# Reloaded products placed earlier, early operands split together, loads of phase two reordered, last norms a stretch later, in a one-layer hybrid trunk

## The chip, the cores and the metric

The kernel runs on one core of a Trainium2 chip. The metric is device time in microseconds (us) of one execution, taken as the median of several. The engines are TensorE (PE; its weight loads are listed apart as PEld), VectorE (DVE), ScalarE (ACT), GpSimd (POOL) and SyncE (SP, which issues most of the DMAs). Each engine works through its own instructions in the order in which they were written; engines wait for each other by semaphores.

## What is computed

The reference is one decoder layer on 1024 tokens of width 1024. Four mixer groups (convolution, latent attention, pooling, spatial gating) make up the first third of the time and are not touched. What matters here is the end:

```python
h = h + mixed @ w_out[l]
f = jnp.square(jax.nn.relu(rms_norm(h, ffn_norm_g[l]) @ w_ff1[l]))   # 1024 x 4096
h = h + f @ w_ff2[l]                                                # 1024 x 1024
return rms_norm(h, final_norm_g)
```

## The kernel before

**Precision.** Every float32 operand is split into a high part (ACT copies it to the format that TensorE reads) and a low part (DVE subtracts the high part from the value). A product takes three passes: high x high, high x low, low x high (`mm3`).

**Seven products instead of eight.** Both matrix products of the MLP are done in 2x2 blocks with seven block products (Strassen's scheme in Winograd's form). The tokens fall into a first and a second half, the 1024 features into two halves, and the 32 tiles of the hidden layer into 16 *pairs* (`Pair`, weights `a11`, `a12` from the first tile of a pair, `a21`, `a22` from the second). The seven products of a pair are P1 to P7. One product is four blocks of features by three passes, 12 matmuls of 128x512; I call these 12 matmuls a **stretch**.

**The order by hand.** All of the MLP is a list `steps` of `Step` objects, one stretch each, put out by `run` (L887 on) in a fixed order, the queue order of every engine. In turn `k` of its loop come, in this order: the loads of step `k+8`; the `post` of step `k-1` (what is done with its result); `prep(k+4)`, that is the high halves on ACT, then the low halves on DVE, then the operand sums of step `k+4`; the functions in the list `now` of step `k`; the `split` of step `k-1` (a result split into halves and stored); the `pre` of step `k`; and the matmuls of step `k`. So operands are made four stretches ahead, and ACT or DVE standing still in a turn hold up all that they have to do in later turns.

**Early pairs.** While the last attention blocks run, only the first half of the tokens is ready. So for the first 12 pairs (`NEARLY`) P1 and P2 are done first (`Pair.early`, L980 on): `one` computes P1 with `a11` into a PSUM bank `ffe`; its `post` copies it to the tile `m` (two buffers, tag `M`) and stores it to DRAM (`m1[p]`); `two` adds P2 with `a12` into the same bank; its `post` makes the square of the ReLU (`fe`), which is stored whole and, split into halves (`fst`), a second time. The order is one(0), one(1), two(0), one(2), two(1), and so on, so that two(p) follows one(p) three steps later. `a11` and `a12` lie in one raw tile `w_raw` of 512 KB (tag `raw`, two buffers). The split operands `wop` and the stored halves `fst` share ten slots (tag `w`). In the same turns the sums and differences of the second half of the tokens are made, in `now` of the steps 7 to 22 (`hn_T1`, `hn_T1_split`, `combine`, `combine_split`, four of each; `hn_T1` also puts eight transposes on PE, tile `htb`).

**Pairs.** Then come the other five products of pairs 0 to 11, in the order P6(p), P3(p), P7(p), P5(p+1), P4(p). P6, P7 and P4 add up in a PSUM bank `ffx` (tag `W`, two banks), which begins with the stored P1: `load_m1` brings it back to the tile `s1` (tag `e`, one buffer) and `seed` (L1009) copies it into the bank on ACT. P5 and P3 add up in a bank `ffy`. The `post` of P5 keeps it as `s5` (tag `N`, one buffer), that of P6 keeps its bank as `s2` before P7 adds to it, that of P7 adds `s5` and stores, that of P4 takes ReLU and square. Pairs 12 to 15 have all seven products in a row and need no stored P1.

**Phase two.** The second matrix product (`Chunk`, L1086 on) has four chunks of four pairs, each with M1, M2, M4, M6, M5, M7, M3 in this order, and each of these with four token tiles in the order `JS` = 0, 2, 1, 3: 28 stretches a chunk. M1, M6 and M7 use banks `ffa`, the others `ffb`. After each stretch DVE adds the bank to a tile of `h` (`add_h`, L1080). M1, M2 and M4 take stored halves (loads 0, 1, 3 into `fop`), the others sums of the whole values (`f1`, `f2` into `raw_f`); `w1`, `w2` are the weights (`raw_b`). All of these loads are issued by SP, in `now` of some step. The second half of `h` waits in DRAM meanwhile (`h_away`, `h_back`).

**Last norms.** `final(t)` (L1234 on) makes the last norm of a token tile: square and sum on ACT, mean and power -0.5 on POOL, product with factor and gain on DVE, store. In the last chunk M7 finishes tiles 4 to 7, M3 tiles 0 to 3; `final` stands in the `post` of those steps. The very last stretch (`final_tile`) is cut into two quarters of 256 columns, the second of which writes the same bank as the first and so waits for DVE's sum of the first.

The lines of the profile that come up: L160 all matmuls of `mm3`; L878 and L881 high and low half of an operand; L130 and L131 those of a stored result; L977 the copies `m`, `s2`, `s5`; L1011 the seed; L946 ReLU; L948 its square on DVE; L967, L1015, L1102, L1108 the loads of `w_raw`, `s1`, `fop`, `raw_b` and `raw_f`; L1018 to L1027 the sums of a pair's weights; L1237 to L1241 the last norm.

Of the kernel before, what the change touches and what calls it, by code (L numbers as in the profile page):

```python
# [7 lines left out]
F32 = mybir.dt.float32  # L8
# [7 lines left out]
P = 128  # L16
# [61 lines left out]
def _trunk(tc, nc, act, dve, pool, pe, sb, ps, hbm, a):  # L78
# [768 lines left out]
    def slot(name):  # L847
        return wslot(name).rearrange("p (x c) -> p x c", x=2)

    def E(name):  # L850
        return sb.tile([P, 512], F32, tag="e", name=name, bufs=1)

# [75 lines left out]
            nc.sync.dma_start(hs[t], h[4 + t])  # L928

    def h_back():  # L930
        for t in range(4):
            h[4 + t] = U("P", "h_back", [D])
            nc.sync.dma_start(h[4 + t], hs[t])

# [26 lines left out]
    class Pair:  # L961
# [18 lines left out]
        def early(self):  # L980
            p = self.p
            o1, o2 = self.op("a11"), self.op("a12")

            def one():
                self.bx = (W, K, W, O)[p % 4]("ffe")
                mm_half(self.bx, o1.t, "B11", True)

            def one_post():
                self.keep("m1", lambda n: M(n, [512]), self.bx)
                pool.dma_start(m1[p], self.m1)  # L990

            def two():
                mm_half(self.bx, o2.t, "B21", False)

            def two_post():
                self.f = (E if p % 2 == 0 and p < NEARLY - 4 else N)("fe")
                f_relu(p, 0, self.bx, self.f, True)

            def two_split():
                f_parts(p, 0, self.f, slot("fst") if p > 2 else  # L1000
                        sb.tile([P, 2, 512], F32R, tag="CS", name="fst", bufs=1))

            return (Step(one, [o1], loads=[lambda: self.load(0)], post=one_post),
                    Step(two, [o2], post=two_post, split=two_split))

        def banks(self):
            self.bx = W("ffx")
# [21 lines left out]
        def steps(self):  # L1029
            p, whole = self.p, self.p >= NEARLY  # L1030
            S = {}

            def product(name, wop, bank, tok, start, **kw):
                o = self.op(wop)
                S[name] = Step(lambda: mm_half(bank(), o.t, tok, start), [o], **kw)

            def y0():
                self.by = (K, O)[p % 2]("ffy")
                return self.by

            def x():
                return self.bx

            def z_seed():
                self.bz = X("ffz")[:, 0:512]
                if p < NEARLY + 2:
                    set_bank(self.bz)
                act.activation(self.bz, self.bx, AF.Copy)

            def two_post():  # L1050
                self.f11 = E("f11")
                f_relu(p, 0, self.bz, self.f11, False)

            def four_post():
                self.f21 = M("f21", [512])
                f_relu(p, 1, self.bx, self.f21, False)

            load = [lambda: self.load(0, "H"), lambda: self.load(1)]
            if whole:
                product("P1", "a11", x, "B11", True, loads=load, pre=self.banks, post=z_seed, sums=[self.sum1])  # L1060
                load = []
                product("P2", "a12", lambda: self.bz, "B21", False, sums=[self.sum4], post=two_post,
                        split=lambda: f_parts(p, 0, self.f11, slot("fst")))
            product("P5", "a21", y0, "T1", True, loads=load, sums=[self.sum2],
                    post=lambda: self.keep("s5", N, self.by))
            product("P6", "a11", x, "T2", False, pre=None if whole else self.seed, sums=[] if whole else [self.sum4],
                    post=lambda: self.keep("s2", lambda n: M(n, [512]), self.bx))
            product("P3", "a12", lambda: self.by, "B22", False, sums=[] if whole else [self.sum3],
                    post=lambda: f_sum(p, 2, self.by, self.s2))
            product("P7", "a21", x, "T3", False, post=lambda: f_sum(p, 3, self.bx, self.s5),  # L1070
                    split=lambda: f_parts(p, 3, self.s5, slot("fst")))
            product("P4", "a22", x, "T4", False, post=four_post, split=lambda: f_parts(p, 1, self.f21, slot("fst")))
            if whole:
                S["P2"].sums.append(self.sum3)
            self.S = S
# [8 lines left out]
    class Chunk:  # L1084
# [65 lines left out]
        def steps(self, nxt, first):  # L1150
            S = {}
            for m, (bank, start, f, w, to) in self.SPEC.items():
                wops = [Op(w_slot, lambda w=w, i=i: self.r[w, i]) for i in range(NCH)]
                fops = [Op(lambda: unit("B", "fop"), lambda f=f, i=i: self.r[f, i]) for i in range(NCH)]

                def fop(i, f=f, fops=fops):
                    return self.r[f, i] if isinstance(f, int) else fops[i].t

                for n, j in enumerate(JS):
                    def pre(m=m, bank=bank, n=n):  # L1160
                        if n == 0 and m in ("M1", "M2", "M4", "M5"):
                            self.banks(bank)

                    def mm(bank=bank, start=start, j=j, fop=fop, wops=wops):
                        for i in range(NCH):
                            mm3(getattr(self, bank)[j], lambda x: fop(i)[:, x, j * P:(j + 1) * P],
                                lambda y: wops[i].t[:, y, :], start and i == 0, i == NCH - 1, not start)

                    def post(m=m, bank=bank, j=j, n=n, to=to):
                        for t, half in to:  # L1170
                            add_h(t + j, half, getattr(self, bank)[j])
                        if self.last and m == "M7" and n < 2:
                            final(4 + j)
                        if self.last and m == "M3":
                            final(j)
                            if n < 2:
                                final(4 + JS[n + 2])

                    if self.last and m == "M3" and n == 3:
                        mm = lambda fop=fop, wops=wops: final_tile(fop, wops, self.B[3])  # L1180
                        post = None
                    S[m, n] = Step(mm, [wops[n]] + ([] if isinstance(f, int) else [fops[n]]), pre=pre, post=post)
# [6 lines left out]
            for n in range(4):  # L1189
# [7 lines left out]
                now(*ahead_4[n], self.sum("S2", n))  # L1197
                now("M6", n, self.sum("T3", n))
                now("M5", n, self.sum("S4", n))
                now("M1", n, self.ld(1, n))  # L1200
                now("M2", n, self.ld(3, n))
                if nxt:
                    now("M4", n, nxt.ld(0, n))
# [4 lines left out]
    def final_tile(fop, wops, b):  # L1208
# [3 lines left out]
        for n, (lo, hi) in enumerate(pieces):  # L1212
            if n:
                sl = slice(lo - 512, hi - 512)
                for i in range(NCH):
                    mm3(b[:, sl], lambda x: fop(i)[:, x, t * P:(t + 1) * P], lambda y: wops[i].t[:, y, sl],
                        False, i == NCH - 1, True)
                add_h(t, 1, b[:, sl], lo - 512, hi - 512)
            act.activation(jk[:, lo:hi], h[t][:, lo:hi], AF.Square, accum_out=ssq[:, n:n + 1])  # L1219
            pool.tensor_scalar(ms[:, n:n + 1], ssq[:, n:n + 1], 1.0 / D, epsr[:, t:t + 1] if n == 0 else ms[:, n - 1:n],  # L1220
                               ALU.mult, ALU.add)
# [9 lines left out]
        fin["g"] = sb.tile([P, D], F32, tag="CS", name="gain_fin", bufs=1)  # L1231
        nc.sync.dma_start(fin["g"], a["fin_g"].partition_broadcast(P))

    def final(t):  # L1234
        jk = M("fjunk", [512]).bitcast(BF16)
        ssq = small(1, "mssq")
        act.activation(jk, h[t], AF.Square, accum_out=ssq)  # L1237
        ms, rs = small(1, "mr_ms"), small(1, "mr_rs")
        pool.tensor_scalar(ms, ssq, 1.0 / D, epsr[:, t:t + 1], ALU.mult, ALU.add)  # L1239
        pool.tensor_tensor(rs, ms, nhalf[:, 0:1], ALU.pow)  # L1240
        dve.scalar_tensor_tensor(h[t], h[t], rs, fin["g"], ALU.mult, ALU.mult)  # L1241
        nc.sync.dma_start(a["out"][t], h[t])


# [231 lines left out]
    for p in range(NPAIR):  # L1476
# [6 lines left out]
            steps.append(s["P4"])  # L1483
        else:
            steps += [s[n] for n in ("P1", "P5", "P6", "P2", "P7", "P3", "P4")]
        if p + 1 < NEARLY:
            steps[-3 if p + 2 < NEARLY else -2].now.append(pairs[p + 1].load_m1)
    steps[2 * NEARLY - 6].now.append(pairs[0].load_m1)
    tail, tail2 = steps[-7:], steps[-14:-7]
    c0 = chunks[0]  # L1490
    for t, n, name, ii in ((tail2, 1, "w1", (0, 1)), (tail2, 5, "w1", (2,)), (tail, 2, "w1", (3,)),
                           (tail, 2, 0, range(4)), (tail, 3, "w2", range(4)), (tail, 5, "f1", range(4)), (tail, 6, "f2", range(4))):
        t[n].now += [c0.ld(name, i) for i in ii]
    for n in range(4):
        tail[3 + n].now.append(c0.sum("T1", n))
    for c, ch in enumerate(chunks):
        steps += ch.steps(chunks[c + 1] if c + 1 < len(chunks) else None, c == 0)
    steps[-28 * len(chunks) + 3].now.append(h_back)
    steps[-20].now.append(load_gain)
    run(steps)  # L1500


# [105 lines left out]
```

## Time and profile before

| what | us |
|---|---|
| median of 3 runs (lowest, highest) | 1131.64 (1131.16, 1134.97) |
| the profiled execution, its own time | 1135.26 |
| its span, first to last instruction | 1133.5 |
| mean granted TensorE clock | 0.957 of full speed |
| early pairs, from the second `m` copy to the first seeded product | 395.8 to 500.1 |
| pairs 0 to 11, from P6(0) to P6(11) | 500.1 to 696.2 |
| phase two | 786.0 to 1133.5 |

A row of a timeline gives start, duration, engine, line of the kernel, operation, output <- inputs, shapes and number, and in brackets how long the engine had stood idle before it and what ended that wait. A row of a wait list gives the total, the number of times and the longest. PE's durations overlap, since a matmul begins before the one ahead of it has ended: the start of the next row tells the pace.

### The profile page before, as it was taken

Reading aid. Unit: us, or ns where it says so; the run is one execution under the profiler, and the core shown is the slowest. Engines: PE = TensorE matmul, PEld = TensorE weight load, DVE = VectorE, ACT = ScalarE, POOL = GpSimd, SP = SyncE. Lnnn points to the kernel's source line nnn. Section 1 sums busy time; section 2 is a strip of 40 time slices with the busy share of each in tenths; the row PEclk is TensorE's granted clock in tenths of the full one; section 3 lists DMA queues with packets and bytes.
Section 4 is the critical chain, followed back from the end, with each engine's and each line's share of the span. In section 5 each row is a group of like instructions: output and inputs, shape, how many; then the busy total and the mean of one; then the engine's idle time right before and its main releaser. Section 6 shows DMA issues by size and latency. Waiting matters only on the chain. (4 is left out here: it accounts for less than half of the span.)

```text
span 1133.5 us, 13377 instructions
## 1 busy us (share of the span) xinstructions
PE 1016.8 (90%) x4674; PEld 830.9 (73%) x4674; DVE 848.0 (75%) x1276; ACT 499.9 (44%) x936; POOL 245.0 (22%) x333
## 2 busy tenths in 40 slices
PE   9977799999999996667878878999799999999993
PEld 7866688878888885546766666888588888888872
DVE  5999999988887546655546555567698988988874
ACT  7552266566577644444344343554143241431422
POOL 0478666213323221111111111112000000000002
PEclk9998899999999998879899899999899999999996
DMA  9311034101010054845454545458929248166002
GB/s 343 116 48 45 19 105 169 39 19 38 1 57 1 1 184 148 319 165 178 169 179 180 186 159 184 177 194 336 413 81 356 105 152 298 71 236 228 1 37 112
DMA packets 49492, 165.71 MB, mean 146 GB/s; under 512 B 6032, under 2 KB 7952, under 8 KB 49424
## 3 DMA queue, kind: packets, MB, share of 16 engines
q1 hardware_dynamic: 36288, 119.68, 30.0%
q0 software_dynamic: 12992, 45.10, 10.4%
q8 instruction: 37, 0.61, 0.2%
q14 instruction: 31, 0.25, 0.1%
q10 hardware_dynamic: 144, 0.07, 0.0%
HBM read 113.45 MB, written 51.38 MB: 145 GB/s over the span
## 5 line engine op out<-in xcount | busy, mean ns | idle before, releaser
L160 PE MATMUL ffb<-wop,fop 128*128 128x512 f32 (+1 forms) x780 | 185.7, 399 | 19.1 <-DVE h L1080 11.1
L160 PE MATMUL ffx<-hnT,wop 128*128 128x512 f32 x624 | 162.1, 412 | 41.4 <-ACT ffx L1011 40.6
L160 PEld LDWEIGHTS ffb<-wop,fop 128*128 128x128 f32 x780 | 147.7, 193 | 55.5 <-DVE h L1080 11.3
L881 DVE TENSOR_TENSOR wop<-w_raw,wop 128x512 fp32r<-128x512 f32 x112 | 77.0, 689 | 144.8 <-ACT wop L878 144.7
L160 PEld LDWEIGHTS ffx<-hnT,wop 128*128 128x128 f32 x624 | 123.0, 199 | 74.1 <-ACT ffx L1011 45.7
L160 PE MATMUL ffa<-wop,fop 128*128 128x512 f32 x576 | 136.9, 397 | 2.0 <-DVE h_back L1080 2.0
L160 PEld LDWEIGHTS ffa<-wop,fop 128*128 128x128 f32 x576 | 109.3, 190 | 27.7 <-DVE h_back L1080 2.4
L878 ACT ACTIVATE wop<-raw_b 128x512 fp32r<-128x512 f32 x96 | 59.4, 623 | 127.8 <-PE ffa L160 40.0
L878 ACT ACTIVATE wop<-w_raw 128x512 fp32r<-128x512 f32 x112 | 69.7, 625 | 80.9 <-DMA w_raw<-in_w_ff 34.2
L337 DVE SCALAR_TENSOR_TENSOR acc<-ycv,cols,acc 128x512 f32<-128x512 f32 (+22 forms) x100 | 97.0, 1012 | 0.7 <-ACT acc L317 0.4
L160 PE MATMUL ffe<-hnT,wop 128*128 128x512 f32 x288 | 77.2, 425 | 20.3 <-ACT m L977 20.3
L160 PEld LDWEIGHTS ffe<-hnT,wop 128*128 128x128 f32 x288 | 57.8, 205 | 36.4 <-ACT m L977 23.7
L1239 POOL TENSOR_SCALAR mr_ms<-mssq,epsr 128x1 f32<-128x1 f32 x7 | 3.9, 564 | 322.3 <-ACT fjunk L1237 322.1
L878 ACT ACTIVATE fop<-raw_f 128x512 fp32r<-128x512 f32 x64 | 39.8, 623 | 76.4 <-DVE h_back L1080 27.6
L881 DVE TENSOR_TENSOR wop<-raw_b,wop 128x512 fp32r<-128x512 f32 x96 | 65.5, 683 | 5.5 <-ACT wop L878 5.0
L955 POOL DMA_DIRECT2D fs<-fst x48 | 25.9, 539 | 103.6 <-DVE fst L131 100.1
L160 PE MATMUL ffy<-hnB,wop 128*128 128x512 f32 x192 | 47.2, 395 | 0.0
L160 PE MATMUL ffy<-hnT,wop 128*128 128x512 f32 x192 | 46.5, 391 | 0.0
L881 DVE TENSOR_TENSOR fop<-raw_f,fop 128x512 fp32r<-128x512 f32 x64 | 43.8, 685 | 0.0
L937 POOL DMA_DIRECT2D fr<-s x32 | 17.3, 542 | 121.1 <-DVE s L942 121.1
L160 PEld LDWEIGHTS ffy<-hnB,wop 128*128 128x128 f32 x192 | 36.8, 192 | 8.4
L160 PEld LDWEIGHTS ffy<-hnT,wop 128*128 128x128 f32 x192 | 36.0, 188 | 7.9
(448 smaller groups left out, 2167.7 us busy)
## 6 DMA issues: line engine op xcount, KB each, us to landing
fs<-fst POOLq DMA_DIRECT2D x48, 512.0 KB, 3.6
fop<-fs SPq DMA_DIRECT2D x48, 512.0 KB, 7.1
w_raw<-in_w_ff SPq DMA_DIRECT2D x44, 512.0 KB, 4.7
raw_b<-in_w_ff SPq DMA_DIRECT2D x32, 512.0 KB, 5.4
raw_f<-fr SPq DMA_DIRECT2D x32, 512.0 KB, 5.6
fr<-s POOLq DMA_DIRECT2D x32, 256.0 KB, 2.3
fr<-f POOLq DMA_DIRECT2D x20, 256.0 KB, 2.4
xin<-in_x SPq DMA_DIRECT2D x8, 512.0 KB, 8.8
```

Of the source, the lines that this page charges most:

```text
L160: pe.matmul(out, lhs(x), rhs(y), start=start and i == 0, stop=stop and i == 2, skip_group_check=more)
L337: dve.scalar_tensor_tensor(aa, ya, c, aa, ALU.mult, ALU.add)
L878: act.activation(self.t[:, 0], self.src(), AF.Copy)
L881: dve.tensor_sub(self.t[:, 1], self.src(), high(self.t))
L937: pool.dma_start(fr[p][q // 2][:, (q % 2) * 512:(q % 2 + 1) * 512], f)
L955: pool.dma_start(fs[p][q], t.rearrange("p x c -> p (x c)").bitcast(F32))
L1239: pool.tensor_scalar(ms, ssq, 1.0 / D, epsr[:, t:t + 1], ALU.mult, ALU.add)
```

## The change

Six things change:

- An early pair's two operands, `a11` and `a12`, are both operands of `one`; `two` has none. So both are split in the same turn, four stretches ahead of `one`.
- `seed` of pair p moves from the `pre` of its own P6 to `now` of P7 of pair p-1 (pair 0: to `now` of its P5). `load_m1` of pair p moves from `now` of P7(p-1) to `now` of P4(p-2) (pair 1: to P6(0)).
- `s5` of odd pairs goes to a second buffer (tag `CS`) by a new function `spare`.
- The four loads of kind 1 of the first chunk are issued in `tail[3]` (P2 of the last pair), ahead of the four of `w2`, instead of one in each step of M1. `h_back` goes from M1's last step to M2's last, that is behind the loads of kind 3, and in the order `JS`.
- `final` is cut in two: `final_sum` (ACT and POOL) in the turn in which the tile is finished, after that turn's operands, and `final_out` (the product and the store), one turn or more later.
- Tile 4's product goes to ACT and POOL instead of DVE; those of tiles 2 and 1 stand inside `final_tile`, each behind the sum of a quarter.

```diff
+    def spare(name):
+        return sb.tile([P, 2, 512], F32, tag="CS", name=name, bufs=1)[:, 0]
...
     def h_back():
-        for t in range(4):
+        for t in JS:
...
-            return (Step(one, [o1], loads=[lambda: self.load(0)], post=one_post),
-                    Step(two, [o2], post=two_post, split=two_split))
+            return (Step(one, [o1, o2], loads=[lambda: self.load(0)], post=one_post),
+                    Step(two, post=two_post, split=two_split))
...
-                    post=lambda: self.keep("s5", N, self.by))
-            product("P6", "a11", x, "T2", False, pre=None if whole else self.seed, sums=[] if whole else [self.sum4],
+                    post=lambda: self.keep("s5", (N, spare)[p % 2], self.by))
+            product("P6", "a11", x, "T2", False, sums=[] if whole else [self.sum4],
...
-                        if self.last and m == "M7" and n < 2:
-                            final(4 + j)
-                        if self.last and m == "M3":
-                            final(j)
-                            if n < 2:
-                                final(4 + JS[n + 2])
...
-                now("M1", n, self.ld(1, n))
+                if not first:
+                    now("M1", n, self.ld(1, n))
                 now("M2", n, self.ld(3, n))
...
                 add_h(t, 1, b[:, sl], lo - 512, hi - 512)
+                final_out((2, 1)[n - 1])
...
-    def final(t):
+    def final_sum(t):
         jk = M("fjunk", [512]).bitcast(BF16)
         ssq = small(1, "mssq")
         act.activation(jk, h[t], AF.Square, accum_out=ssq)
-        ms, rs = small(1, "mr_ms"), small(1, "mr_rs")
+        ms, fin[t] = small(1, "mr_ms"), small(1, "fin_rs", 4)
         pool.tensor_scalar(ms, ssq, 1.0 / D, epsr[:, t:t + 1], ALU.mult, ALU.add)
-        pool.tensor_tensor(rs, ms, nhalf[:, 0:1], ALU.pow)
-        dve.scalar_tensor_tensor(h[t], h[t], rs, fin["g"], ALU.mult, ALU.mult)
+        pool.tensor_tensor(fin[t], ms, nhalf[:, 0:1], ALU.pow)
+
+    def final_out(t, shared=False):
+        if shared:
+            act.activation(h[t], h[t], AF.Copy, scale=fin[t])
+            pool.tensor_tensor(h[t], h[t], fin["g"], ALU.mult)
+        else:
+            dve.scalar_tensor_tensor(h[t], h[t], fin[t], fin["g"], ALU.mult, ALU.mult)
         nc.sync.dma_start(a["out"][t], h[t])
...
-        if p + 1 < NEARLY:
-            steps[-3 if p + 2 < NEARLY else -2].now.append(pairs[p + 1].load_m1)
     steps[2 * NEARLY - 6].now.append(pairs[0].load_m1)
+    pairs[0].S["P5"].now.append(pairs[0].seed)
+    for p in range(1, NEARLY):
+        (pairs[0].S["P6"] if p == 1 else pairs[p - 2].S["P4"]).now.append(pairs[p].load_m1)
+        pairs[p - 1].S["P7"].now.append(pairs[p].seed)
...
-                           (tail, 2, 0, range(4)), (tail, 3, "w2", range(4)), (tail, 5, "f1", range(4)), (tail, 6, "f2", range(4))):
+                           (tail, 2, 0, range(4)), (tail, 3, 1, range(4)), (tail, 3, "w2", range(4)),
+                           (tail, 5, "f1", range(4)), (tail, 6, "f2", range(4))):
...
-    steps[-28 * len(chunks) + 3].now.append(h_back)
+    steps[-28 * len(chunks) + 7].now.append(h_back)
     steps[-20].now.append(load_gain)
+
+    for k, t in ((-7, 4), (-6, 6), (-5, 5), (-4, 7), (-3, 0), (-2, 2)):
+        steps[k - 1].split = lambda t=t: final_sum(t)
+    for k, t in ((-5, 4), (-4, 6), (-3, 5), (-2, 7), (-1, 0)):
+        steps[k].now.append(lambda t=t: final_out(t, t == 4))
+    steps[-2].split = lambda: final_sum(1)
```

## The prediction

> **What bounds the kernel now.** I read the page's first two parts, then what TensorE waited for, then a table by stage.
>
> ```profile
> span 1133.5 us, 13377 instructions
> ## 1 busy us (share of the span) xinstructions
> PE 1016.8 (90%) x4674; PEld 830.9 (73%) x4674; DVE 848.0 (75%) x1276; ACT 499.9 (44%) x936; POOL 245.0 (22%) x333
> ```
>
> TensorE (PE) is the bound on average, so only its waits are worth anything. The list of waits, from the last mixer products on (total, times, longest):
>
> ```profile
> PE ffx L160 <- ACT ffx L1011: 40.6, 12, 9.0
> PE ffe L160 <- ACT m L977: 20.3, 8, 5.4
> PE ffb L160 <- DVE h L1080: 11.1, 1, 11.1
> PE ffb L160 <- DMA fop<-fs: 8.0, 1, 8.0
> PE ffa L160 <- DVE h_back L1080: 2.0, 1, 2.0
> ```
>
> These five are 82.0 us, and each is touched by one part of the change. The windows by stage (length, then busy us of PE, PEld, DVE, ACT, POOL, then granted clock, DMA share, GB/s):
>
> ```profile
> 395.80:500.10 104.30, 75.79 (x308) 59.39 (x308) 63.10 (x101) 48.17 (x87) 19.98 (x37) 0.89 0.57 206
> 500.10:696.20 196.10, 164.46 (x661) 130.65 (x661) 105.94 (x164) 75.66 (x132) 29.21 (x54) 0.94 0.51 177
> ...
> 786.00:830.20 44.20, 36.18 (x145) 28.53 (x144) 32.22 (x51) 12.63 (x23) 1.62 (x3) 0.88 0.86 347
> 830.20:1086.90 256.70, 256.70 (x1105) 207.52 (x1104) 229.44 (x356) 82.66 (x148) 0.00 (x0) 1.00 0.47 166
> 1086.90:1133.50 46.60, 26.15 (x109) 20.73 (x107) 24.34 (x32) 12.59 (x26) 9.10 (x18) 0.76 0.23 91
> ```
>
> The fourth row is what is possible: 92 stretches in 256.7 us, 2.79 each, at clock 1.00. In the other four TensorE waits and its clock is lower; a wait costs itself and some slow matmuls behind it.
>
> **Part 1, early pairs: both operands split together.**
>
> ```profile
> 395.81 14.10 PE L160 MATMUL ffe<-hnT,wop 128*128 128x512 f32 x60 [0.75 <-ACT m L977]
> 409.75 1.03 PE L793 MATMUL htb<-ident,h 128*128 128x128 f32 x8
> ...
> 446.82 0.63 ACT L878 ACTIVATE wop<-w_raw 128x512 fp32r<-128x512 f32 x1 [4.94 <-DMA w_raw<-in_w_ff]
> ...
> 447.49 0.69 DVE L881 TENSOR_TENSOR wop<-w_raw,wop 128x512 fp32r<-128x512 f32 x1 [3.54 <-ACT wop L878]
> ...
> 453.15 0.69 DVE L948 TENSOR_TENSOR fe<-fe 128x512 f32<-128x512 f32 x1
> ...
> 477.98 0.60 ACT L977 ACTIVATE m<-ffe 128x512 f32<-128x512 f32 x1 [4.17 <-DMA m<-m]
> ...
> 484.72 0.60 ACT L977 ACTIVATE m<-ffe 128x512 f32<-128x512 f32 x1 [0.44 <-DMA m<-m]
> ...
> 495.81 0.63 ACT L878 ACTIVATE wop<-w_raw 128x512 fp32r<-128x512 f32 x1 [1.36 <-DVE w_raw L1018]
> ...
> 500.11 4.73 PE L160 MATMUL ffx<-hnT,wop 128*128 128x512 f32 x12 [8.98 <-ACT ffx L1011]
> ```
>
> ACT stands 4.94 us on a weight load, and behind it, in order, is the copy `m` for which TensorE waits. The load is late because the two raw buffers are freed only when the second operand is split, in the loop turn before the one that needs the next load. Split together, the buffer is free three turns earlier and the load has four turns, some 11 us: this wait goes. No instruction is added; ten operand slots are enough by count (seven held, one or two for the stored products).
>
> What is late next is DVE: 447.49 to 453.84 is ten operations without a gap, 6.3 us for two stretches, against 2 x 2.76 plus 0.8 of transposes, 6.3, on TensorE (five stretches from 395.81 to 409.75 give 2.79). So in the turns with the first hidden-half sums they are even; in the last four pairs of turns DVE has nine to eleven operations, 6.4 to 7.6 us against 5.5, and the copy `m` can meet its buffer still being stored (the 4.17). I put the lag by the last `m` at 8 us (estimate: 4 x about 1.2, and one or two waits of half of 4.17). Dense, TensorE would reach that point at 395.81 + 20 x 2.757 + 4 x 0.8 = 454.1, so the last `m` comes at about 462.5 and not 484.72. Bounds: 454.1, and 484.7 with no gain.
>
> From there to the first `ffx` product it was 15.4 us (500.11 - 484.72). The seed now follows the operand at 495.81 at once: 495.81 + 0.53 + 0.59 gives 497.0 in that frame, 12.3 after `m`. So that product starts at 474.8 and not 500.1: **25 us** gained, bounds 33 and 3.
>
> **Part 2, the seeds, the second s5 buffer.**
>
> ```profile
> 521.56 2.91 PE L160 MATMUL ffy<-hnB,wop 128*128 128x512 f32 x12
> ...
> 529.83 2.88 PE L160 MATMUL ffx<-hnT,wop 128*128 128x512 f32 x12
> 535.58 3.03 PE L160 MATMUL ffx<-hnT,wop 128*128 128x512 f32 x12 [2.87 <-ACT ffx L1011]
> ...
> 552.49 5.49 PE L160 MATMUL ffx<-hnT,wop 128*128 128x512 f32 x12 [2.87 <-ACT ffx L1011]
> ```
>
> ```profile
> 531.40 0.60 ACT L977 ACTIVATE s<-ffy 128x512 f32<-128x512 f32 x1 [2.04 <-DMA fr<-s]
> ...
> 532.74 0.60 ACT L946 ACTIVATE f<-ffx 128x512 f32<-128x512 f32 x1 [0.22 <-PE ffx L160]
> ...
> 534.95 0.58 ACT L1011 ACTIVATE ffx<-s 128x512 f32<-128x512 f32 x1
> ```
>
> Three stretches from 521.56 to 529.83 are 2.757 each. P4 ends near 532.6; ACT then does ReLU, square, an operand and the store's high half, and only then the seed at 534.95, for which P6 waits: 2.87 us in every pair, now and then with a slow stretch behind (5.49). The seed moves to the turn of P7 of the pair before, three turns ahead of its P6. It needs the other of two W banks, read last by ReLU one period back, and `s1` loaded:
>
> ```profile
> s<-m SPq DMA_DIRECT2D x12, 256.0 KB, 4.5
> ```
>
> The one `s1` buffer is free when the previous seed is done, and the load stands in SP's queue behind no load that waits longer; it has almost a period, 13.8 us, for 4.5. So P6 starts at once. Next late would be the copy `s2` between P6 and P7: ACT's four operations after P4 ended by 534.95 without the seed, 2.3 us into a stretch of 2.76, so it is in time. Behind the waiting seed on ACT would be operands four turns ahead, so its own 0.58 is hidden. The second `s5` buffer takes away the 2.04, but ReLU then began 0.22 after TensorE anyway: 0 as long as ACT has this 0.2 us, and at most 2 a pair if not.
>
> Eleven periods of five stretches are 151.6 us and were 196.1: 44.5, of which I keep **44** (bounds 44.5, and 33 if 1 us a pair comes back).
>
> **Part 3, first loads of phase two.**
>
> ```profile
> 771.54 0.33 SPq L1108 DMA_DIRECT2D raw_b<-in_w_ff  x1
> ...
> 805.06 25.33 PE L160 MATMUL ffb<-wop,fop 128*128 128x512 f32 x96 [8.02 <-DMA fop<-fs]
> ```
>
> ```profile
> 800.00:804.00 4.00, 0.00 (x0) 0.00 (x0) 1.90 (x3) 0.63 (x1) 0.00 (x0) 0.59 1.03 420
> ```
>
> M2 waits 8.02 us for four loads at the end of the queue, and runs slow behind it. Dense, M1, M2 and M4 would take 12 x 2.79 = 33.5 of the 44.2: 10.7 to gain. But the DMA engines are full (share 1.03, 420 GB/s): reordering moves the lateness. Before M2 now stand 13 loads of 0.52 MB and about 3 MB of stores, 9.8 MB from 771.5 on: at 420 GB/s, 23.4, and a little slower at first, 797; the last operand behind it 798.5, so M2 waits 1 to 2 us. Eight loads for the sums (4.2 MB, 10 us) and four for M4 (2.1 MB, 5 us) end at 812, when M2 would be done at 810. So some 2.5 us come back there: M6 at 824 and not 830.2, **6 us** (bounds 10.7 and 0). `h_back` moves behind these four loads and lands by 818, its first tile (JS order) by 813.5; M4's first sum needs it at 815.
>
> **Part 4, last norms.**
>
> ```profile
> 1101.90 10.26 PE L160 MATMUL ffb<-wop,fop 128*128 128x512 f32 x48
> 1123.22 2.93 PE L160 MATMUL ffb<-wop,fop 128*128 128x256 f32 x12 [11.07 <-DVE h L1080]
> ```
>
> ```profile
> 1115.18 1.28 DVE L1241 SCALAR_TENSOR_TENSOR h<-h,mr_rs,gain_fin 128x1024 f32<-128x1024 f32 x1 [2.27 <-POOL mr_rs L1240]
> ...
> 1126.19 0.48 DVE L1080 SCALAR_TENSOR_TENSOR h<-ffb,rs,h 128x256 f32<-128x256 f32 x1 [3.02 <-PE ffb L160]
> ```
>
> DVE stands 2.27 us in each norm for the chain square, mean, power, so the sum that the last 256-column product waits for comes 11.07 us late; the 2.0 before the last M7 tile (list of waits) is the same queue. A turn later the factor is there: DVE has one or two sums of a half tile, some 0.75 each (below twice the 0.48 of a quarter), and 1.28 of a norm in a stretch of 2.79. From 1086.93: seven stretches to 1106.5, 1.4 for the first quarter, DVE free at 1108.7 (a sum and a norm from 1106.5), its sum 0.5, the last product 1.4 and 0.2, so its sum begins at 1110.9 and not 1126.19. Behind it the same 7.3 us to the end, plus 0.6 where a norm on DVE holds the last mean on POOL, as here:
>
> ```profile
> 1109.00 1.30 POOL L1239 TENSOR_SCALAR mr_ms<-mssq,epsr 128x1 f32<-128x1 f32 x1
> ...
> 1120.55 0.27 POOL L1239 TENSOR_SCALAR mr_ms<-mssq,epsr 128x1 f32<-128x1 f32 x1 [3.33 <-ACT fjunk L1237]
> ```
>
> (1.30 beside a norm on DVE, 0.27 without.) So 1118.8: **14.5 us** (bounds 16 and 10). Tile 4's norm goes to ACT and POOL; nearest is POOL's 128x1024 subtraction, 3.00 us, off the path if DVE is free of it.
>
> ```profile
> L148 POOL TENSOR_TENSOR wo_1l<-wo_raw,wo_1h 128x1024 fp32r<-128x1024 f32 x2 | 6.0, 2998 | 2.7 <-ACT wo_1h L147 2.7
> ```
>
> [...]
>
> **Sum.** 25 + 44 + 6 + 14.5 = 89.5; 1133.5 - 89.5 = 1044.0, and the execution's 1135.3 was 1.8 over its span: **1046**. That execution lies 3.6 over the median of 1131.6; I read this as slow stretches behind waits, which go, and take nothing off.
>
> **Rivals.**
> - A, the early pairs stay bound by DVE and the stores of `m`, some 8 us a pair: for it, DVE is even with TensorE and the 4.17; against it, DVE was idle 3.5 us a pair. It gives back 12 to 25: 1058 to 1071. Chance 0.18.
> - B, another wait in each pair (`s2` before P7): 1 to 3 us by eleven, 1057 to 1079; against it, P7 never waited. 0.06.
> - C, the loads of phase two only move the wait, DMA being full: 1052. 0.08.
> - D, the seeds do not take their wait away, since another copy ends at the same place: 1090. 0.03.
> - E, slower than before: `s1` lands late, and ACT, in order, holds everything behind the seed. It costs landing time over 13.8 us, by eleven; to lose 89.5 it must land after 22 us, against 4.5. 1140. 0.03.
> - Forecast, all four within their bounds: 0.62, from 1033 (33 + 44.5 + 10.7 + 16 less a little) to 1056.
>
> The range takes the forecast, C and most of A: 1033 to 1066. A measurement of this kernel tells 0.3% from no change; faster 0.95, same 0.02, slower 0.03 (E).
>
> **What would show it.** Right: no wait `ffx <- ACT L1011`, five stretches of 2.76 a pair, the wait `m <- DMA w_raw` gone with the early pairs near 79 us, M2 waiting under 3 us, the last product within 2 us of the one before. Wrong: ACT waiting for DVE or for `m` stores in the early turns, a wait of P7, DVE waiting for POOL in the last turns, M4 waiting for `fop`.

## The result, and the profile after

The changed kernel takes 1051.82 us (median, 1050.52 to 1054.26); beside it the kernel before took 1132.11 (1131.16 to 1134.97). The ratio is 0.9289, with a 95% interval of 0.9265 to 0.9313. The forecast was 1046, with a range of 1033 to 1066.

The page of the changed kernel begins:

```profile
span 1048.7 us, 13388 instructions
## 1 busy us (share of the span) xinstructions
PE 996.6 (95%) x4674; PEld 819.9 (78%) x4674; DVE 845.9 (81%) x1275; ACT 503.4 (48%) x937; POOL 247.0 (24%) x334
```

The same number of instructions on every engine, give or take one, in a span 84.8 us shorter. The windows by stage, cut at the same instructions as before (length, then busy us of PE, PEld, DVE, ACT, POOL, then granted clock, DMA share, GB/s):

```profile
395.72:478.50 82.78, 69.72 (x309) 55.81 (x309) 60.15 (x97) 46.57 (x84) 19.35 (x36) 0.97 0.70 250
478.50:632.24 153.74, 153.74 (x661) 125.61 (x662) 106.81 (x165) 76.34 (x131) 29.10 (x54) 0.99 0.66 224
...
721.90:760.87 38.97, 35.20 (x145) 28.14 (x144) 30.77 (x49) 11.18 (x19) 1.61 (x3) 0.96 0.98 394
760.87:1017.60 256.73, 256.73 (x1106) 207.51 (x1105) 230.53 (x359) 85.39 (x153) 0.00 (x0) 1.00 0.46 166
1017.60:1048.70 31.10, 22.85 (x109) 18.63 (x107) 23.58 (x31) 12.59 (x25) 12.98 (x19) 0.96 0.35 136
```

| stage | before | after | saved | forecast |
|---|---|---|---|---|
| early pairs, to the first `ffx` product | 104.3 | 82.8 | 21.5 | 25 |
| eleven pair periods | 196.1 | 153.7 | 42.4 | 44 |
| M1 to M6 of the first chunk | 44.2 | 39.0 | 5.2 | 6 |
| M6 to the last M7 | 256.7 | 256.7 | 0 | 0 |
| from the last M7 to the end | 46.6 | 31.1 | 15.5 | 14.5 |

The gain of 84.6 in these rows is all of the span's 84.8: nothing was given back elsewhere. What TensorE still waits for behind the mixers (total, times, longest):

```profile
PE ffe L160 <- ACT m L980: 8.8, 5, 3.2
PE ffx L160 <- ACT ffx L1014: 5.0, 1, 5.0
PE ffa L160 <- DVE h L1083: 3.8, 1, 3.8
PE ffb L160 <- DVE h L1083: 1.0, 1, 1.0
```

82.0 us in the five lines shown before, 18.6 in these four. (Lines of the code past the first edit stand three lower: the copy L977 is now L980, the seed L1011 now L1014, the sum L1080 now L1083.) The wait for the seed, twelve times before, is left once, at the first stored product. The wait of 3.8 in M1 is new.

The pairs in TensorE's timeline (start, length, tiles, count, idle before):

```profile
478.50 5.12 PE L160 MATMUL ffx<-hnT,wop 128*128 128x512 f32 x12 [5.03 <-ACT ffx L1014]
483.45 2.90 PE L160 MATMUL ffy<-hnB,wop 128*128 128x512 f32 x12
...
491.71 5.65 PE L160 MATMUL ffx<-hnT,wop 128*128 128x512 f32 x24
497.19 2.93 PE L160 MATMUL ffy<-hnB,wop 128*128 128x512 f32 x12
```

The row of 24 matmuls is P4 of one pair and P6 of the next without a gap; from 483.45 to 497.19 is a whole period of five stretches, 13.74 us. ACT's rows of the copy `m`, the last four of the early pairs:

```profile
443.86 0.60 ACT L980 ACTIVATE m<-ffe 128x512 f32<-128x512 f32 x1 [6.29 <-DMA m<-m]
...
451.31 0.60 ACT L980 ACTIVATE m<-ffe 128x512 f32<-128x512 f32 x1 [2.30 <-DMA m<-m]
...
459.48 0.60 ACT L980 ACTIVATE m<-ffe 128x512 f32<-128x512 f32 x1 [3.07 <-DMA m<-m]
...
465.69 0.58 ACT L980 ACTIVATE m<-ffe 128x512 f32<-128x512 f32 x1
```

Three of the four stand on the store of an earlier `m`: only two buffers hold it, and they also serve the sums `hb_raw4`. The new wait of M1, in the timeline of all engines:

```profile
728.00 0.63 ACT L881 ACTIVATE wop<-raw_b 128x512 fp32r<-128x512 f32 x1 [4.64 <-DMA raw_b<-in_w_ff]
...
728.66 0.69 DVE L884 TENSOR_TENSOR wop<-raw_b,wop 128x512 fp32r<-128x512 f32 x1 [5.04 <-ACT wop L881]
...
730.47 0.75 DVE L1083 SCALAR_TENSOR_TENSOR h<-ffa,rs,h 128x512 f32<-128x512 f32 x1
...
731.27 7.36 PE L160 MATMUL ffa<-wop,fop 128*128 128x512 f32 x24 [3.77 <-DVE h L1083]
```

ACT, then DVE, stand in order on a weight load of M2 that now comes behind M2's operands; behind them on DVE is the sum of M1's first tile, and for its bank TensorE waits.

### The profile page after: what moved, and what is told of

Same layout as the page of the kernel before. It is cut to its first block, busy times and chain, and to the rows that moved or that the text cites. A ratio compares the mean times of both kernels' runs of the same rounds, so it can differ in the third digit from the quotient of the medians.

```text
span 1048.7 us, 13388 instructions
## 1 busy us (share of the span) xinstructions
PE 996.6 (95%) x4674; PEld 819.9 (78%) x4674; DVE 845.9 (81%) x1275; ACT 503.4 (48%) x937; POOL 247.0 (24%) x334
## 4 chain that ended last, share of the span: by engine, by line
PE 65%; DVE 15%; issue 8%; DMA 6%; POOL 3%; ACT 3%; SPq 0%; POOLq 0%; DVEq 0%; ACTq 0%
PE ffb L160 17%; PE ffx L160 13%; PE ffa L160 12%; PE ffy L160 8%; DVE acc L337 8%; PE wo L160 4%; PE ob L160 2%; PE s L676 2%; DMA raw_b<-in_w_ff 1%; PE ptb L719 1%; PE woa L160 1%; DMA xin<-in_x 1%; PE qb L160 1%; DMA wp_raw<-in_w_cm 1%; DVE h L475 1%
## 5 line engine op out<-in xcount | busy, mean ns | idle before, releaser
L160 PE MATMUL ffb<-wop,fop 128*128 128x512 f32 (+1 forms) x780 | 181.4, 392 | 1.0 <-DVE h L1083 1.0
L160 PEld LDWEIGHTS ffb<-wop,fop 128*128 128x128 f32 x780 | 145.2, 188 | 35.5 <-DVE h L1083 1.2
L160 PE MATMUL ffx<-hnT,wop 128*128 128x512 f32 x624 | 151.6, 396 | 5.8 <-ACT ffx L1014 5.0
L160 PEld LDWEIGHTS ffx<-hnT,wop 128*128 128x128 f32 x624 | 118.5, 190 | 33.1 <-ACT ffx L1014 5.5
L881 ACT ACTIVATE wop<-raw_b 128x512 fp32r<-128x512 f32 x96 | 59.5, 623 | 123.6 <-PE ffa L160 38.4
L337 DVE SCALAR_TENSOR_TENSOR acc<-ycv,cols,acc 128x512 f32<-128x512 f32 (+22 forms) x100 | 99.6, 1038 | 0.6 <-ACT acc L317 0.3
L160 PE MATMUL ffe<-hnT,wop 128*128 128x512 f32 x288 | 71.1, 402 | 8.8 <-ACT m L980 8.8
L160 PEld LDWEIGHTS ffe<-hnT,wop 128*128 128x128 f32 x288 | 54.2, 192 | 22.4 <-ACT m L980 10.9
L329 POOL TENSOR_TENSOR acc<-acc,tap 128x512 f32<-128x512 f32 (+7 forms) x20 | 35.2, 1760 | 29.0 <-ACT tap L328 27.7
```

Source lines behind the costliest of these rows:

```text
L160: pe.matmul(out, lhs(x), rhs(y), start=start and i == 0, stop=stop and i == 2, skip_group_check=more)
L329: pool.tensor_tensor(aa, aa, tap, ALU.add)
L337: dve.scalar_tensor_tensor(aa, ya, c, aa, ALU.mult, ALU.add)
L881: act.activation(self.t[:, 0], self.src(), AF.Copy)
```

## The experiments

The sets ran on different chips, where the kernel before had medians of 1133.0, 1137.7, 1136.8 and 1137.2; the changed kernel itself ran only beside its own result. Differences of 1 or 2 us are therefore read from the stages of the traces and not from the medians. Where an edit leaves a stage alone, its length still varies from run to run: the early pairs take 82.0 to 83.2 us in seven such runs, and M1 to M6 of the first chunk 38.4 to 41.9 in nine, the changed kernel among both.

### Each part undone

**early_undone**

```diff
-            return (Step(one, [o1, o2], loads=[lambda: self.load(0)], post=one_post),
-                    Step(two, post=two_post, split=two_split))
+            return (Step(one, [o1], loads=[lambda: self.load(0)], post=one_post),
+                    Step(two, [o2], post=two_post, split=two_split))
```

> The changed kernel with only part 1 undone: the two operands of an early pair are again taken in two turns. If the parts are worth what the windows say and add up, it is 21 us slower than the changed kernel, 1073 us, the weight-load wait of ACT is back in the early turns, and everything behind the first ffx product takes as long as in the changed kernel. If the 21 us came from the seeds (a seed two stretches ahead would hide a late early stage), undoing this costs under 10 us: below 1062.

1071.24 us (1068.87 to 1073.07), 19.4 more. ACT's list of waits in the early stage has the weight load back:

```profile
ACT wop L881 <- DMA w_raw<-in_w_ff: 33.9, 8, 5.5
...
ACT m L980 <- DMA m<-m: 4.4, 3, 3.8
```

Note the second line: with the weight loads late, the stores of `m` hold ACT 4.4 us; in the changed kernel 11.7. The one wait had covered part of the other. The early pairs take 101.6 us (397.48 to 499.09) instead of 82.8.

**seeds_undone**: the seed is issued ahead of its P6 again, and the loads of the stored products stand where they stood; the second `s5` buffer stays.

```diff
+        if p + 1 < NEARLY:
+            steps[-3 if p + 2 < NEARLY else -2].now.append(pairs[p + 1].load_m1)
...
-    pairs[0].S["P5"].now.append(pairs[0].seed)
-    for p in range(1, NEARLY):
-        (pairs[0].S["P6"] if p == 1 else pairs[p - 2].S["P4"]).now.append(pairs[p].load_m1)
-        pairs[p - 1].S["P7"].now.append(pairs[p].seed)
...
-            product("P6", "a11", x, "T2", False, sums=[] if whole else [self.sum4],
+            product("P6", "a11", x, "T2", False, pre=None if whole else self.seed, sums=[] if whole else [self.sum4],
```

> The changed kernel with the seeds and the loads of the stored products at their old places, and the second s5 buffer kept. If the seed's wait is all of part 2, the eleven periods go from 151.6 to 193 to 196 us and the time is 1092 to 1096. If the second s5 buffer carries a part, the wait for ffx is shorter than 2.87 us a pair and the time is 1070 to 1088.

1095.93 us (1093.92 to 1098.06), 44.1 more. TensorE's list of waits:

```profile
PE ffx L160 <- ACT ffx L1014: 41.6, 12, 9.5
```

Eleven times 2.9 and one of 9.5, as in the kernel before (40.6, 12, 9.0), with two `s5` buffers as with one. The eleven periods take 194.9 us (483.42 to 678.27) instead of 153.7: the seed's place is all of part 2. The early pairs take 85.7 instead of 82.8; that is the first seed, which the prediction counts in part 1.

**loads_undone**

```diff
-                if not first:
-                    now("M1", n, self.ld(1, n))
+                now("M1", n, self.ld(1, n))
...
-                           (tail, 2, 0, range(4)), (tail, 3, 1, range(4)), (tail, 3, "w2", range(4)),
+                           (tail, 2, 0, range(4)), (tail, 3, "w2", range(4)),
...
-    steps[-28 * len(chunks) + 7].now.append(h_back)
+    steps[-28 * len(chunks) + 3].now.append(h_back)
```

(`h_back` also takes its tiles in plain order again.)

> The changed kernel with the loads of M2's operands and of the second half of h at their old places. If the stage's gain is the order of the loads, M2 waits some 8 us again and the time is 1057 (5 us more). If the order does not matter because the DMA engines are full either way, it is within 2 us of the changed kernel: 1050 to 1054.

1055.54 us (1055.02 to 1056.35), 3.7 more. TensorE's timeline:

```profile
721.46 11.04 PE L160 MATMUL ffa<-wop,fop 128*128 128x512 f32 x48
740.55 25.22 PE L160 MATMUL ffb<-wop,fop 128*128 128x512 f32 x96 [8.05 <-DMA fop<-fs]
765.61 11.36 PE L160 MATMUL ffa<-wop,fop 128*128 128x512 f32 x48
```

M1 runs dense, M2 waits 8.05 us for `fop`, and M1 to M6 takes 44.15, 5.2 more; this run's first `ffx` product came 1.1 sooner, at 477.4. The order of the loads is worth 2.3 to 5.8 us here, by the spread of 38.4 to 41.9 for this stage in the nine runs that leave it alone; in these M1 waits once, 3.4 to 5.5 us, and M2 does not.

**tail_undone**: `final_sum` and `final_out` called together where `final` was, all on DVE.

> The changed kernel with the last norms in one piece, at their old places, all on DVE. If the chain of square, mean and power inside DVE's queue was the whole loss, the last product waits some 11 us for its sum again and the time is 1067 (15.5 us more). If the tail's gain came in part from earlier ends of the stages ahead of it (h loads landing sooner), it is less: under 1062.

1067.13 us (1065.77 to 1068.49), 15.3 more. TensorE's waits have the two lines of the kernel before again:

```profile
PE ffb L160 <- DVE h L1083: 11.0, 1, 11.0
...
PE ffa L160 <- DVE h_back L1083: 2.0, 1, 2.0
```

The four parts cost 19.4 + 44.1 + 3.7 + 15.3 = 82.5 when undone one by one; together they gained 80.3. They add, to within the spread of these medians: nothing here says that a part works only because another is there.

### What a part of the change is worth by itself

**s5_single**

```diff
-                    post=lambda: self.keep("s5", (N, spare)[p % 2], self.by))
+                    post=lambda: self.keep("s5", N, self.by))
```

> The changed kernel with one s5 buffer for all pairs, as before. By my reading the second one buys nothing: the copy then waits some 2 us for its buffer, but the ReLU behind it still begins within 0.2 us of the end of TensorE's stretch, and the seed is three stretches away: within 1.5 us of the changed kernel, 1050 to 1053. If the wait holds ACT long enough to delay the copy s2 of the next stretch, it costs up to 2 us in each of eleven pairs: 1062 to 1074.

1050.74 us (1049.97 to 1052.41): no difference. The wait that the second buffer removes is there, 26.2 us of it in the list of ACT's waits between 485 and 630, and its timeline shows where it ends:

```profile
ACT s L980 <- DMA fr<-s: 26.2, 10, 4.0
```

```profile
535.68 0.60 ACT L980 ACTIVATE s<-ffy 128x512 f32<-128x512 f32 x1 [2.27 <-DMA fr<-s]
...
536.79 0.60 ACT L949 ACTIVATE f<-ffx 128x512 f32<-128x512 f32 x1
```

ACT goes on to the ReLU without a pause, and TensorE's periods stay at 13.77 us (five stretches, 533.87 to 547.64). ACT is not the bound here, and its 26.2 us of waiting cost nothing.

**tail4_dve**

```diff
-        steps[k].now.append(lambda t=t: final_out(t, t == 4))
+        steps[k].now.append(lambda t=t: final_out(t))
```

> The changed kernel with the norm of tile 4 on DVE like the others, and not on ACT and POOL. If POOL's 2.9 us and the DVE norm it stretches (1.83 instead of 1.28) cost nothing at the end, as they are seven stretches ahead of it, DVE's extra 1.3 us is the same size and the time is within 1 us of the changed kernel. If the shared norm is what keeps DVE ahead of the last products, the last sums come 1 to 1.5 us later: 1052.5 to 1053.5. [...]

1051.31 us (1050.31 to 1053.22): no difference. From the last M7 to the end is 31.1 us (1018.40 to 1049.5), as with the shared norm. The division of that norm between ACT and POOL is worth nothing, and its price is nothing. That price can be seen in the changed kernel's last turns all the same:

```profile
1028.15 2.91 POOL L1244 TENSOR_TENSOR h_back<-h_back,gain_fin 128x1024 f32<-128x1024 f32 x1 [1.16 <-ACT h_back L1243]
...
1030.32 1.83 DVE L1246 SCALAR_TENSOR_TENSOR h_back<-h_back,fin_rs,gain_fin 128x1024 f32<-128x1024 f32 x1
...
1033.24 1.40 POOL L1239 TENSOR_TENSOR fin_rs<-mr_ms,nhalf 128x1 f32<-128x1 f32 x1
...
1038.06 1.28 DVE L1246 SCALAR_TENSOR_TENSOR h<-h,fin_rs,gain_fin 128x1024 f32<-128x1024 f32 x1
...
1041.50 0.48 DVE L1083 SCALAR_TENSOR_TENSOR h<-ffb,rs,h 128x256 f32<-128x256 f32 x1 [0.58 <-PE ffb L160]
```

(L1244 is POOL's product of the shared norm, L1246 a norm on DVE, L1239 the power, L1083 the last sum.) A norm on DVE beside POOL's product took 1.83 and not 1.28, a power on POOL beside a norm 1.40 and not 0.54 (the median of seven); the last sum begins 23.9 us after the start of the last M7 with the shared norm (1041.50) and without it (1042.28).

### What is left of the early stage

It took 82.8 us and the forecast's lower bound was 104.3 - 33 = 71. Three runs ask what the rest is: DVE's rows (rival A's first half) or stores of the early pairs (its second half).

**m_cs**

```diff
-                self.keep("m1", lambda n: M(n, [512]), self.bx)
+                self.keep("m1", spare if p > 3 and p % 2 else lambda n: M(n, [512]), self.bx)
```

> The changed kernel with the stored product m of the odd early pairs from pair 5 on in a buffer of its own, so that three hold these products instead of two. If the rest of the early stage is the store of m (three waits of ACT, 11.7 us), these go, the early stage falls from 82.8 to about 76 us and the time to 1043 to 1047. If DVE is what paces those turns, ACT waits for DVE instead and the time stays within 2 us of the changed kernel.

1047.73 us (1047.03 to 1049.46). The early pairs take 78.2 us (397.66 to 475.85) instead of 82.8. ACT's waits for a store of `m` are gone (11.7 to 0.3), and another store, that of `fe`, has taken part of their place:

```profile
ACT fe L949 <- DMA fr<-fe: 5.4, 2, 3.4
```

In the changed kernel that line says 2.0, once. Neither theory was right as it stood: the stores were a cause, but of two kinds.

**away_spread**: the four stores of the second half of `h` in turns 6, 8, 10 and 12 and not all in turn 14.

```diff
-    def h_away():
-        for t in range(4):
-            nc.sync.dma_start(hs[t], h[4 + t])
+    def h_away(t):
+        nc.sync.dma_start(hs[t], h[4 + t])
...
-    steps[14].now.append(h_away)
+    for t in range(4):
+        steps[6 + 2 * t].now.append(lambda t=t: h_away(t))
```

> The changed kernel with the stores of the second half of h, four of 512 KB that go out in one turn at 432, put into turns 6, 8, 10 and 12 (some 408 to 427), where the DMA engines are 0.6 to 0.8 busy. If the stores of m are slow because they stand behind these 2 MB, ACT waits for m stores at most once and briefly, and the time falls as with a third buffer for m: 1046 to 1049. If they are slow for another reason (the stores of the early pairs themselves), ACT waits some 11 us for m again and the time is within 1.5 us of the changed kernel.

1046.14 us (1045.00 to 1047.47). The early pairs take 80.3 us (395.42 to 475.69) instead of 82.8. In the list of ACT's waits (lines stand one higher in this kernel):

```profile
ACT m L979 <- DMA m<-m: 8.4, 3, 3.5
...
ACT fst L130 <- DMA fs<-fst: 5.0, 2, 3.3
```

The longest wait for `m` fell from 6.3 to 3.5, the sum only from 11.7 to 8.4, and the wait for `fst` grew from 1.1 to 5.0. The 2 MB of `h` explain the worst of these waits, not all of them. The time is that of the first theory, the waits are between the two, and the early pairs gave only 2.5 us of the 5.7 between the two medians.

**free_buffers**: more buffers for these stores. `m` of pairs 5, 7 and 9 goes to a third one, `fe` goes to two by turns to the end, and the first stored product is reloaded into the spare one, two turns later.

```diff
-                self.keep("m1", lambda n: M(n, [512]), self.bx)
+                self.keep("m1", spare if p in (5, 7, 9) else lambda n: M(n, [512]), self.bx)
...
-                self.f = (E if p % 2 == 0 and p < NEARLY - 4 else N)("fe")
+                self.f = (E if p % 2 == 0 else N)("fe")
...
-            self.s1 = E("s1")
+            self.s1 = (E if self.p else spare)("s1")
...
-    steps[2 * NEARLY - 6].now.append(pairs[0].load_m1)
+    steps[2 * NEARLY - 4].now.append(pairs[0].load_m1)
```

> The changed kernel with buffers for the stores of the early pairs: m of pairs 5, 7 and 9 in a third buffer, the sums fe by turns in two buffers to the end, and the first stored product reloaded into the spare buffer, a turn later. If stores hold the early stage up and nothing else does, ACT waits for no store there, no wait of TensorE for m is left, and the first ffx product starts 5 to 8 us sooner than in the changed kernel: 1044 to 1047. If DVE is next behind the stores, as its dense rows from 454 to 471 in the run with m alone in a third buffer say, TensorE still waits 2 to 5 us for m with ACT waiting for DVE, and the gain over that run is at most 2 us: 1046 to 1049.

1042.24 us (1039.57 to 1042.99; ratio to the kernel before 0.9159, interval 0.9141 to 0.9177). TensorE in the early turns:

```profile
429.37 27.85 PE L160 MATMUL ffe<-hnT,wop 128*128 128x512 f32 x120
458.58 3.04 PE L160 MATMUL ffe<-hnT,wop 128*128 128x512 f32 x12 [1.36 <-ACT m L980]
...
468.21 4.61 PE L160 MATMUL ffx<-hnT,wop 128*128 128x512 f32 x12 [3.87 <-ACT ffx L1014]
```

Ten stretches without a gap, and the early pairs take 72.7 us (395.47 to 468.21), 10.0 less than in the changed kernel: more than either theory gave. ACT's waits for stores of `m` are down to 1.5. DVE's list of waits between 436 and 470:

```profile
DVE hnT L827 <- ACT hnT L825: 2.8, 4, 0.7
DVE wop L884 <- ACT wop L881: 1.4, 2, 0.7
```

DVE stands still for 4.2 of 34 us, never over 0.7 at a time, so it does come next; but with it TensorE waits 1.36 for `m` and 3.87 for the first seed, and no longer.

### The first loads of phase two

**w2_first**

```diff
-                           (tail, 2, 0, range(4)), (tail, 3, 1, range(4)), (tail, 3, "w2", range(4)),
+                           (tail, 2, 0, range(4)), (tail, 3, "w2", range(4)), (tail, 3, 1, range(4)),
```

> The changed kernel with one exchange in SP's queue: the four loads of the second weight half ahead of the four operands of M2, and not behind them. If the rest of that stage is the lateness of those weights (M1's third tile waits 3.77 us for a sum that stands on DVE behind them), the wait goes and M2 is still in time, its operands landing by about 729 against a start at 733: M1 to M6 takes 34 to 35 instead of 39.0, time 1047 to 1048. If the DMA engines only hand the lateness on, M2 waits 2 to 4 us instead and the time is within 1.5 us of the changed kernel.

1052.68 us (1049.12 to 1053.08): no gain. TensorE's timeline:

```profile
722.00 11.04 PE L160 MATMUL ffa<-wop,fop 128*128 128x512 f32 x48
...
747.43 0.94 PE L160 MATMUL ffb<-wop,fop 128*128 128x512 f32 x3 [2.18 <-DMA fop<-fs]
...
763.04 11.36 PE L160 MATMUL ffa<-wop,fop 128*128 128x512 f32 x48
```

M1 runs without its wait, and M2 waits 0.5 in two pieces. But M4 now waits for its operands (2.18, then 0.34 twice) and M6 starts 41.0 us after M1 instead of 39.0, no gain and, with 38.4 to 41.9 in runs that leave this stage alone, no clear loss. The second theory holds in its mechanism, with another victim than it named.

**k1_sooner**

```diff
-                           (tail, 2, 0, range(4)), (tail, 3, 1, range(4)), (tail, 3, "w2", range(4)),
+                           (tail, 1, 1, range(4)), (tail, 2, 0, range(4)), (tail, 3, "w2", range(4)),
```

> The changed kernel with the four operands of M2 loaded one stretch after the last use of their buffers, ahead of those of M1, so that the DMA engines, a third busy from 690 to 704, are full some 2.5 us sooner. If the loads' total holds the first stretches of phase two, all that follows lands some 2.5 us sooner and M1 to M6 takes 36.5 instead of 39.0: 1048 to 1050. If DVE's own row of sums holds that stage, nothing changes: 1051 to 1053.

1049.12 us (1048.77 to 1051.44). M1 to M6 takes 37.9 (721.28 to 759.17): 1.1 less than in the changed kernel (2.5 was expected), but only 0.5 under the shortest of the nine runs that leave the stage alone. A gain is therefore not shown. Two windows of the changed kernel say why one was looked for:

```profile
690.00:704.00 14.00, 14.00 (x63) 11.45 (x61) 9.39 (x15) 6.50 (x12) 1.73 (x4) 1.00 0.28 110
708.00:756.00 48.00, 44.23 (x186) 35.59 (x185) 34.05 (x53) 15.11 (x26) 3.77 (x7) 0.96 1.02 400
```

The DMA engines are 0.28 busy, and then full for 48 us. Within these an exchange of two loads moves the wait, as `w2_first` shows; that an earlier start helps all was argued and is not shown. The waits that are left are 1.93 and, for `fop`, 0.5 in M1 and 1.0 in M4.

**both**: the last two edits together.

> The two edits of the other runs of this set together. If each works in its own stage, the gains add: 1041 to 1045. If the sooner loads only make the wait another one, it is as fast as the kernel with the free buffers alone.

1039.82 us (1038.95 to 1043.26; ratio 0.9148, interval 0.9128 to 0.9168), the fastest kernel here. M1 to M6 is 38.2 (712.71 to 750.89) against 38.8 with the free buffers alone; the two intervals overlap, so that the second edit adds anything to the first is not shown.

## Why the prediction was right

The forecast was 5.8 us under the median. By the spans, 1044.0 against 1048.7, it is 4.7: the four parts gave 3.5, 1.6 and 0.8 less and 1.0 more than forecast. The rest is that the profiled execution (1050.5) lies below the median of its kernel. Two things in this agreement are luck. The forecast was taken from an execution 3.6 above its kernel's median, with nothing taken off, because slow stretches behind waits would go; but the times of the changed kernel spread as widely (1050.52 to 1054.26), and by the medians the change gave 80.3, so that is not shown. And the median lies on rival C's 1052, though not for its reason: the stage that C speaks of saved 5.2.

- **Part 1, right in its mechanism, one term mis-sized.** The wait for the weight load went (`early_undone` brings 33.9 us of it back, and it was 34.2 in the kernel before), and TensorE runs dense to 443. The last `m` came at 465.69 and not 462.5, and the first `ffx` product 12.8 behind it and not 12.3. The lag behind a dense TensorE was put at 8 us: 4 x 1.2 for DVE and one or two waits of half of 4.17 for stores. The first was near enough: with more buffers (`free_buffers`) the last `m` comes 62.5 after the start of the stage (395.47 to 457.93), 4.1 behind the dense 58.3. The second was the mis-sized one: without these buffers it comes after 70.0 (395.72 to 465.69), so stores cost 7.5, not 2 to 4. The 4.17 was read from a trace in which late weight loads gave most stores time to end (`early_undone`: 4.4 in all), and the buffers that were in time at that pace were late at the new one (11.7). Rival A had this mechanism, and at a price of 12 to 25 was too dear: 3.5 of the 25 were lost, and all that `free_buffers` takes out of the stage is 10.0.
- **Part 2, right.** Twelve waits became one; the periods are 13.77 us. Of the 44.5 that eleven dense periods give, 2.1 are missing, and they stand in the first row: that P6 follows a wait of 5.03 and takes 4.95 to the next start instead of 2.75. That wait is part 1's. The zero for the `s5` buffer was right (`s5_single`), for the reason that was given: ACT needed no more than the slack that it had. Rivals B, D and E did not occur.
- **Part 3, right in size, wrong in place.** 5.2 and not 6 (2.3 to 5.9 by the spread of this stage), but M2 was forecast to wait 1 to 2 and M4 2.5, and neither waits: M1 does, for 3.77 and some 1.8 of slow matmuls. The landing was forecast well: the last of the 13 loads 11 us after the start of M1, and ACT waited for weight halves until 10.2 after it (721.90 to 732.06). The step that failed is what waits for them: the four weight halves among these loads were counted as bytes ahead of M2, and not as what ACT, then DVE, then a bank of M1 stand on. That the size came near all the same is luck: the 5.5 lost in M1, which the forecast does not have, stands in place of 4.7 forecast for M2 and M4. That the DMA engines are full (share 0.98 in this stage) and reordering moves the lateness was right (`w2_first`, and rival C for that run).
- **Part 4, right.** The last sum begins 23.9 us after the start of the last M7 (1017.60 to 1041.50); the forecast's rows gave 24.0. Behind it are 7.2 and not 7.9. Beside POOL's product a norm on DVE took 0.55 more (1.83 against 1.28), and at the end that cost nothing: from the last M7 on 31.1 us with it and without it (`tail4_dve`).

## What to carry to other kernels

Undo a wait and the next one can be a buffer whose reuse had been in time only because of the first (here stores of `m`: 4.4 us of ACT's waits in `early_undone`, 11.7 in the changed kernel): size the stores again at the new pace, and not with the wait that the old trace shows. Where the DMA engines were full (share 1.02 for 48 us in the changed kernel), the order of the loads decided who waited and for how long (M2 for 8.0 us, M1 for 3.8, or M4 for 2.9): follow a load that moves back through every engine that stands on it in order. Before a gain of 1 us in a stage is believed, see how far that stage varies in runs that leave it alone. Two waits in one queue need not add (the 26.2 us of `s5_single` cost nothing): before paying for a buffer, see whether the engine behind it has anything to be late for.

## What the hardware showed

The same wait did not always cost the same. Of the eleven waits of 2.9 us for a seed in the kernel before, seven were followed by a stretch of 3.02 or 3.03 us and four by a longer one. Three of the long ones (the fourth, at 552.49, stands in the prediction) and one other:

```profile
572.09 4.59 PE L160 MATMUL ffx<-hnT,wop 128*128 128x512 f32 x12 [2.87 <-ACT ffx L1011]
590.53 3.03 PE L160 MATMUL ffx<-hnT,wop 128*128 128x512 f32 x12 [2.87 <-ACT ffx L1011]
...
641.23 5.49 PE L160 MATMUL ffx<-hnT,wop 128*128 128x512 f32 x12 [2.90 <-ACT ffx L1011]
660.83 4.59 PE L160 MATMUL ffx<-hnT,wop 128*128 128x512 f32 x12 [2.87 <-ACT ffx L1011]
```

The granted clock of TensorE is the third figure from the end in these two windows, one of a usual stretch and one of a long one:

```profile
535.58:538.45 2.87, 2.87 (x13) 2.36 (x13) 0.27 (x1) 0.00 (x0) 0.54 (x1) 1.00 0.90 257
552.49:557.78 5.29, 5.29 (x13) 4.13 (x13) 0.27 (x1) 0.00 (x0) 0.54 (x1) 0.50 0.87 259
```

A wait of 2.87 to 2.90 us was followed by 3.02 or 3.03, or by 4.59 to 5.49, for the same twelve matmuls; the clock was 1.00 in the stretch at 535.58, 0.50 in the two of 5.49 and 0.62 to 0.63 in the two of 4.59. In `seeds_undone` ten waits of 2.92 were followed by 3.03 eight times, and by 4.56 and 5.49. In the kernel before the long ones come in twos, 88.74 us apart (552.49 to 641.23, and 572.09 to 660.83). What decides whether a long stretch follows is not shown: no run moves such a wait and leaves all else alone.

Whole periods of the kernel before give the price: 16.88 us with a usual stretch behind the wait (518.70 to 535.58), 18.44 and 19.60 with a long one (572.09 to 590.53, 552.49 to 572.09), against 13.79 for five stretches of 2.757. So such a wait cost itself and 0.2 us more, or itself and 1.8 to 2.9 more, and part of what a removed wait gives is this: in `seeds_undone` the eleven periods take 43.3 us more than the dense 151.6, of which 32.1 are waits.
